# A YOCO decoder step: the cross attention's queries stored class by class instead of token by token

## The chip, the cores and the metric

The kernel runs on 1 core of one Trainium2 chip. The metric is the device time of one execution in microseconds (us). Three runs of the kernel before gave 3384.84, 3386.16 and 3391.25 us; the median is 3386.16 us.

## What is computed

The reference is one inference step of a two-layer decoder: a gated linear attention layer, then a cross attention over a shared K/V, each followed by a SwiGLU block. It is done for a prompt of 1024 tokens and for 64 sample tokens (8 sequences of 8) with the same weights. The change lies in the cross attention of the prompt, of which this is the core:

```python
WINDOWS, DILATIONS = (128, 512, 2048), (1, 4, 16)      # three groups, 16 heads each, 4 KV heads, 64 per head

def dilated_group(q, kv, start, dil, n_keys, bias):     # n_keys = window / dilation + 1 = 129
    q_pos = start + arange(Tq)
    idx = q_pos[:, None] - dil * arange(n_keys)[None, :]
    s = einsum('bqhgd,bqkhd->bqhgk', q, k[idx]) * HEAD_DIM ** -0.5
    s = where(idx >= 0, s + bias, -inf)
    p = softmax(s)
    return einsum('bqhgk,bqkhd->bqhgd', p, v[idx]), logsumexp(s)
# q = u @ w_q; the three groups' outputs are mixed with softmax weights of their logsumexp, then @ w_o
```

A query sees only keys at multiples of the dilation, so tokens fall into classes that don't see one another: in the group of dilation 4, the four classes of tokens with the same remainder by 4.

## The kernel before

All products run on TensorE (PE). A product has a left operand that is loaded into the array (LDWEIGHTS, the engine row PEld in the profile) and a right one that is streamed past it (MATMUL, row PE). Every matrix is kept as a high and a low float32r part, and a dense product is three matmuls (`mm3`, lines 164 to 170): high by high, high by low, low by high.

`cross` (line 1529) goes through twelve steps: group 2 (dilation 16), then group 1 (dilation 4), then group 0 (dilation 1), and in each the four KV heads `c`. In a step, `attend` (line 1122) computes the attention of eight tiles of 128 queries, and, woven between its stages by rates written in `cross`, side work runs: `proj_cq` (line 1037) projects the queries of the next step, `sample` serves the sample tokens of the group that was finished last, and, with group 0, `merge` mixes the groups. The order on every engine is fixed when the program is built.

**Projection.** `proj_cq` computes, for each of three token chunks `ch` (384, 384 and 320 columns, the last with 256 prompt tokens) and each half `j` of the four heads, a PSUM tile `ps` of 128 head-dimension rows by the chunk's tokens: 24 matmuls. There are two PSUM banks for these tiles (tag `mm`). The tile is then written to SBUF:
- group 2: one ScalarE (ACT) instruction, line 1060, into a float32 tile `Q` of 128 x 1024;
- groups 1 and 0: `Q` holds 512 tokens and two planes `e`, one per head. For each head ACT writes the rounded high part to its own 64 partitions (line 1070), and VectorE (DVE) writes the remainder to the other 64 (lines 1071 to 1073). One operand thus carries the high and the low part of a query, and the key tile `KT` holds the matching key rows twice.

Within a `Q` tile the tokens lie in their natural order.

**Scores.** `attend` picks the 128 queries of tile `t` out of `Q` (lines 1136, 1148, 1152) and uses them as the left operand (lines 1168, 1170, 1171):

```python
# g == 0                                     128 neighbouring columns
qv = [q[t // 4 * 2 + j][:, :, t % 4 * P:t % 4 * P + P] for j in range(2)]
# g == 1                                     every 4th column
qv = [q[2 * h + j].rearrange("p e (m r) -> p e r m", r=4)[:, :, r] for j in range(2)]
# g == 2                                     every 8th column
qv = [x.rearrange("p (m r) -> p r m", r=8)[:, t] for x in q]
```

In group 2 the prompt is cut into 8 classes of 128 tokens, and the bias masks the keys between; a score is one float32 product of 64 rows (line 1168), which the profile shows as two loads and two matmuls, for the heads `e` = 0 and 1 on the lower and the upper 64 rows of the array. A tile has four such products. In groups 1 and 0 each of the four heads has two products of 128 rows, with the two parts of the keys (lines 1170 and 1171), so eight loads to a tile, over 128 or 256 keys.

After the scores, DVE adds the bias and takes the maximum (line 1175), ACT takes the exponential (1177), PE transposes the probabilities (1200), ACT and DVE split them into `PT` (1202, 1203), PE multiplies by the values (1209), and ACT and DVE write the result (1213, 1216). The score matmuls of tile `t` stand ahead of the transposes of tile `t` - 1.

Of the kernel before, what the change touches and what calls it, by code (L numbers as in the profile page):

```python
# [7 lines left out]
F32 = mybir.dt.float32  # L8
F32R = mybir.dt.float32r
U8 = mybir.dt.uint8  # L10
AF = mybir.ActivationFunctionType
ALU = mybir.AluOpType

P = 128
# [93 lines left out]
class Kern:  # L108
# [928 lines left out]
    def proj_cq(self, u, c, g, q):  # L1037


        nc = self.nc  # L1040
        wq = [self.W.get(x) for x in self.u_cq[c, g]]

        def tile(i):
            while len(q) <= i:
                q.append(self.tl("Q", [P, SEQ]) if g == 2 else self.tl("Q", [P, 2, 512], F32R))
            return q[i]

        for ch, (t0, n) in enumerate(CH):
            n1 = min(n, SEQ - t0)
            for j in range(2):  # L1050
                ps = self.ps("gq")
                for k in range(KD):
                    w = wq[k // 4]
                    js = slice(j * P, (j + 1) * P)
                    self.mm3(ps[:, :n], (w[0][:, k % 4, js], w[1][:, k % 4, js]),
                             (u[k][ch][0][:, :n], u[k][ch][1][:, :n]), k == 0, k == KD - 1)
                    yield
                with self.tc.high_priority():
                    if g == 2:
                        nc.scalar.activation(tile(j)[:, t0:t0 + n1], ps[:, :n1], AF.Copy, scale=0.125)  # L1060
                    else:
                        for h in range(2):
                            a, b = max(t0, h * 512), min(t0 + n1, h * 512 + 512)
                            if a >= b:
                                continue
                            t = tile(2 * h + j)
                            o = slice(a - h * 512, b - h * 512)
                            for e in range(2):
                                hi, lo = slice(e * 64, e * 64 + 64), slice(64 - e * 64, 128 - e * 64)
                                nc.scalar.activation(t[hi, e, o], ps[hi, a - t0:b - t0], AF.Copy, scale=0.125)  # L1070
                                nc.vector.scalar_tensor_tensor(
                                    out=t[lo, e, o], in0=ps[hi, a - t0:b - t0], scalar=0.125,
                                    in1=t[hi, e, o].bitcast(F32), op0=ALU.mult, op1=ALU.subtract)
                    if n1 < n:
                        qn = self.tl("qn", [P, NB * NS])
                        nc.scalar.activation(qn, ps[:, n1:n], AF.Copy, scale=0.125)
                if n1 < n:
                    nc.sync.dma_start(out=self.qs[g][c][2 * j:2 * j + 2].rearrange("e d t -> (e d) t"), in_=qn)
# [43 lines left out]
    def attend(self, c, g, q, load):  # L1122


        nc = self.nc
        mm = nc.tensor.matmul
        bias = next(load)
        kv = [next(load)]
        late = None
        order = (0, 2, 4, 6, 1, 3, 5, 7) if g == 1 else range(8)  # L1130
        rs = self.tl("rs", [P, 8, 8]) if g else None
        for i, t in enumerate(order):
            if i == 1:
                kv.append(next(load))
            if g == 0:
                qv = [q[t // 4 * 2 + j][:, :, t % 4 * P:t % 4 * P + P] for j in range(2)]
                first = max(t - 1, 0)
                nk = 2 if t else 1
                if t % 4 == 0:
                    half = self.wslot("wl").rearrange("p (e n) -> p e n", e=2)  # L1140
                    st = self.tl("st", [P, 3, 4, 8])
                    for x in (1, 2):
                        nc.sync.dma_start(out=st[:, x], in_=self.sts[x][c][t * P:(t + 4) * P].rearrange("(i p) n -> p i n", p=P))
                    self.halves[c].append((half, st))
                out, dst, row = half[:, :, t % 4 * P:t % 4 * P + P], None, st[:, 0, t % 4]
            elif g == 1:
                r, h = t // 2, t % 2
                qv = [q[2 * h + j].rearrange("p e (m r) -> p e r m", r=4)[:, :, r] for j in range(2)]
                first, nk = r * 2, 1 + h
                dst, row = h * 4 + r, rs[:, h * 4 + r]  # L1150
            else:
                qv = [x.rearrange("p (m r) -> p r m", r=8)[:, t] for x in q]
                first, nk = t, 1
                dst, row = t, rs[:, t]
            w = nk * P
            if g:
                out = self.tl("row", [P, 2, P])
            pr = []
            ps = [self.ps("qk") for _ in range(2)]
            runs = [(first, nk)] if first // 4 == (first + nk - 1) // 4 else [(first, 1), (first + 1, 1)]  # L1160
            for hp in range(2):
                for e in range(2):
                    for k0, n in runs:
                        o = ps[e][:, hp * 256 + (k0 - first) * P:hp * 256 + (k0 - first + n) * P]
                        kT, ks = kv[k0 // 4][0], slice(k0 % 4 * P, (k0 % 4 + n) * P)
                        if g == 2:
                            es = slice(e * 64, (e + 1) * 64)
                            m = mm(o, lhsT=qv[hp][es], rhs=kT[es, ks], start=True, stop=True)
                        else:
                            mm(o, lhsT=qv[hp][:, e], rhs=kT[:, 0, ks], start=True, stop=False)  # L1170
                            m = mm(o, lhsT=qv[hp][:, e], rhs=kT[:, 1, ks], start=False, stop=True)  # L1171
            for hq in range(4):
                pv = ps[hq % 2][:, (hq // 2) * 256:(hq // 2) * 256 + w]
                s = self.tl("S", [P, 256])
                nc.vector.tensor_tensor_reduce(s[:, :w], pv, bias[hq][:, :w][:, ::-1], -1.0, 1e38,  # L1175
                                               ALU.add, ALU.min, row[:, hq:hq + 1])
                nc.scalar.activation(s[:, :w], s[:, :w], AF.Exp, bias=row[:, hq:hq + 1], scale=-1.0,
                                     accum_out=row[:, 4 + hq:5 + hq])
                pr.append(s)
            yield m.ins.name  # L1180
            if late:
                yield from late
            late = self.attend_out(c, g, nk, pr, [kv[k // 4][1][:, k % 4] for k in range(first, first + nk)], out, dst)
        yield from late
        if g == 1:
            nc.sync.dma_start(out=self.sts[g][c].rearrange("(h m r) n -> m h r n", h=2, r=4),
                              in_=rs.rearrange("p (h r) n -> p h r n", h=2))
        elif g == 2:
            nc.sync.dma_start(out=self.sts[g][c].rearrange("(m t) n -> m t n", t=8), in_=rs)
# [520 lines left out]
```

## Time and profile before

| | |
|---|---|
| median of three runs | 3386.16 us (3384.84 to 3391.25) |
| the profiled execution, its own time | 3382.68 us |
| its span, first to last instruction | 3380.9 us |
| PE busy | 3301.4 us, 98% |
| PEld (loads of the left operand) busy | 3141.0 us, 93% |
| DVE busy | 1644.9 us, 49% |
| ACT busy | 1219.9 us, 36% |
| cross attention, from the first score product to the last | 1629 to 2444 us |

In the profile a line is L with its number in the kernel, an operand is named without its buffer number (`aux` and `mm` are PSUM banks, `Q` the queries, `KT` the keys), and a shape is partitions by elements; the shape does not tell whether elements are neighbours. Loads and matmuls overlap, so a busy PE is not a PE at its best, and the time that one instruction takes, with its way through the pipeline, is longer than the distance from one to the next. That distance is read from the timeline, as the start of one row less the start of an earlier one. [...]

### The profile page before, as it was taken

The page shows a single profiled execution, that of the slowest core. Times are in us where ns is not written, and L with a number is a line of the kernel's source. Part 1 is how long each engine was busy: PE and PEld are TensorE (multiplying, and loading weights), DVE is VectorE, ACT ScalarE, POOL GpSimd, SP SyncE. Part 2 cuts the span into 40 slices and gives each one's busy share as a digit, 9 for nine tenths or more (in the row PEclk, how much of TensorE's full clock was granted, in tenths as well). Part 3 has the DMA queues.
Part 4 walks back from the last instruction along what each step waited for, and adds up shares of the span by engine and source line. Part 5 has one row for each costly group of instructions (what it writes and reads, how often), then busy time and mean ns, then how long its engine had stood idle before and what let it go on. Part 6 is the DMA issues. An engine that isn't in the chain of part 4 may idle for free. (4 is left out here: it accounts for less than half of the span.)

```text
span 3380.9 us, 51862 instructions
## 1 busy us (share of the span) xinstructions
PE 3301.4 (98%) x20130; PEld 3141.0 (93%) x20130; DVE 1644.9 (49%) x4041; ACT 1219.9 (36%) x3016; POOL 138.2 (4%) x138
## 2 busy tenths in 40 slices
PE   8999999999999999999999999999989999999999
PEld 7899999999999999977889999888878999999998
DVE  5666455533333333652446545767586333333335
ACT  4543344431111111332666555656654211111113
POOL 0000000100000000010000000011111000000000
PEclk9999999999999999999999988989899999999999
DMA  5122234322222222334323333434342322221202
GB/s 182 44 66 75 81 124 150 125 85 94 69 88 87 69 75 94 101 108 142 89 55 113 98 94 97 110 106 120 100 130 99 104 84 85 74 89 63 61 25 110
DMA packets 362410, 318.12 MB, mean 94 GB/s; under 512 B 91208, under 2 KB 346268, under 8 KB 360732
## 3 DMA queue, kind: packets, MB, share of 16 engines
q1 hardware_dynamic: 348472, 302.07, 28.8%
q10 hardware_dynamic: 13596, 12.34, 1.1%
q8 instruction: 158, 2.59, 0.3%
q14 instruction: 88, 0.72, 0.1%
q0 software_dynamic: 96, 0.39, 0.0%
HBM read 251.44 MB, written 107.33 MB: 106 GB/s over the span
## 5 line engine op out<-in xcount | busy, mean ns | idle before, releaser
L166 PE MATMUL aux<-u,wh 128*128 128x384 f32 (+1 forms) x2112 | 696.0, 331 | 2.5 <-ACT u L220 2.5
L169 PE MATMUL aux<-u,wh 128*128 128x384 f32 (+1 forms) x2112 | 695.4, 330 | 0.0
L170 PE MATMUL aux<-u,wl 128*128 128x384 f32 (+1 forms) x2112 | 695.0, 329 | 0.0
L166 PE MATMUL mm<-u,wh 128*128 128x384 f32 (+1 forms) x1152 | 408.8, 355 | 13.4 <-ACT u L220 11.6
L166 PEld LDWEIGHTS aux<-u,wh 128*128 128x128 f32 x2112 | 397.7, 189 | 3.5 <-ACT u L220 3.5
L169 PEld LDWEIGHTS aux<-u,wh 128*128 128x128 f32 x2112 | 397.1, 188 | 0.0
L170 PEld LDWEIGHTS aux<-u,wl 128*128 128x128 f32 x2112 | 397.1, 188 | 0.0
L169 PE MATMUL mm<-u,wh 128*128 128x384 f32 (+1 forms) x1152 | 392.8, 341 | 2.7 <-DVE u L221 2.6
L170 PE MATMUL mm<-u,wl 128*128 128x384 f32 (+1 forms) x1152 | 392.7, 341 | 0.0
L926 DVE TENSOR_TENSOR aux<-g,aux 128x384 f32<-128x384 f32 x132 | 71.3, 540 | 610.9 <-PE aux L170 422.7
L91 ACT ACTIVATE wh<-ws 128x1024 fp32r<-128x1024 f32 (+1 forms) x177 | 184.4, 1052 | 446.8 <-PE aux L169 277.6
L92 DVE TENSOR_TENSOR wl<-ws,wh 128x1024 fp32r<-128x1024 f32 (+1 forms) x177 | 214.2, 1219 | 198.9 <-ACT wh L91 198.3
L166 PEld LDWEIGHTS mm<-u,wh 128*128 128x128 f32 x1152 | 223.7, 194 | 24.4 <-ACT u L220 13.2
L169 PEld LDWEIGHTS mm<-u,wh 128*128 128x128 f32 x1152 | 223.4, 194 | 8.2 <-DVE u L221 4.2
L166 PE MATMUL mm<-h,wh 128*128 128x384 f32 (+1 forms) x704 | 230.4, 328 | 0.0
L170 PE MATMUL mm<-h,wl 128*128 128x384 f32 (+1 forms) x704 | 230.2, 327 | 0.0
L169 PE MATMUL mm<-h,wh 128*128 128x384 f32 (+1 forms) x704 | 230.2, 327 | 0.0
L170 PEld LDWEIGHTS mm<-u,wl 128*128 128x128 f32 x1152 | 223.3, 194 | 2.7 <-issue 0.2
L945 DVE TENSOR_TENSOR y<-y,mm 128x384 f32<-128x384 f32 (+1 forms) x320 | 168.5, 530 | 101.7 <-PE mm L170 101.4
L925 ACT ACTIVATE g<-aux 128x384 f32<-128x384 f32 x132 | 61.8, 468 | 432.4 <-PE aux L170 432.4
L927 ACT ACTIVATE h<-aux 128x384 fp32r<-128x384 f32 x132 | 61.9, 469 | 385.9 <-DVE aux L926 385.9
L1175 DVE CUSTOM_DVE_ANT_0 S<-aux,bias 128x128 f32<-128x128 f32 (+1 forms) x384 | 123.2, 349 | 134.6 <-PE aux L1171 58.7
(311 smaller groups left out, 6149.6 us busy)
## 6 DMA issues: line engine op xcount, KB each, us to landing
ws<-in_w_gate_up_dram SPq DMA_DIRECT2D x88, 512.0 KB
out_dram<-in_cache_win_dram SPq DMA_DIRECT2D x64, 510.0 KB
x<-in_cache_win_dram SPq DMA_DIRECT2D x48, 512.0 KB
ws<-in_w_down_dram SPq DMA_DIRECT2D x44, 512.0 KB
ws<-in_w_in_a_dram SPq DMA_DIRECT2D x24, 512.0 KB
ws<-in_w_q_b_dram SPq DMA_DIRECT2D x24, 512.0 KB
hT<-y SPq DMA_DIRECT2D x48, 192.0 KB
og<-row SPq DMA_DIRECT2D x64, 128.0 KB
```

The source lines that it names most:

```text
L91: nc.scalar.activation(v[1][:, :, :w], v[0][:, :, :w], AF.Copy)
L92: nc.vector.tensor_sub(v[2][:, :, :w], v[0][:, :, :w], v[1][:, :, :w].bitcast(F32))
L166: m = mm(out, lhsT=w[0], rhs=x[0], start=start, stop=False)
L169: mm(out, lhsT=w[0], rhs=x[1], start=False, stop=False)
L170: mm(out, lhsT=w[1], rhs=x[0], start=False, stop=stop)
L925: nc.scalar.activation(t[:, :n], pg[:, :n], AF.Silu)
L926: nc.vector.tensor_mul(pu[:, :n], t[:, :n], pu[:, :n])
L927: nc.scalar.activation(h[:, :n], pu[:, :n], AF.Copy)
L945: nc.vector.tensor_add(ys[m][c][:, :n], ys[m][c][:, :n], ps[:, :n])
L1175: nc.vector.tensor_tensor_reduce(s[:, :w], pv, bias[hq][:, :w][:, ::-1], -1.0, 1e38, ALU.add, ALU.min, row[:, hq:hq + 1])
```

## The change

The queries are written to `Q` class by class. When a projected tile leaves PSUM, the source is read with a step (every 4th column in group 1, every 8th in group 2) and the target is a block of neighbouring columns within each class; the view for group 0 has one class, so nothing changes there. `attend` then takes 128 neighbouring columns as left operand in all groups. Tile sizes, buffers, instruction counts, the order of instructions on every engine and what they wait for are the same; only the shapes of the writes of `Q` differ (128x384 becomes 128x8x48, 64x384 becomes 64x4x96, and so on). In the changed file the lines from `attend_load` on have a number higher by 4, and the three writes are lines 1061, 1074 and 1075.

```diff
                     if g == 2:
-                        nc.scalar.activation(tile(j)[:, t0:t0 + n1], ps[:, :n1], AF.Copy, scale=0.125)
+                        nc.scalar.activation(tile(j).rearrange("p (r m) -> p r m", r=8)[:, :, t0 // 8:(t0 + n1) // 8],
+                                             ps[:, :n1].rearrange("p (m r) -> p r m", r=8), AF.Copy, scale=0.125)
                     else:
                         for h in range(2):
                             a, b = max(t0, h * 512), min(t0 + n1, h * 512 + 512)
                             if a >= b:
                                 continue
-                            t = tile(2 * h + j)
-                            o = slice(a - h * 512, b - h * 512)
+                            r = 4 if g else 1
+                            t = tile(2 * h + j).rearrange("p e (r m) -> p e r m", r=r)
+                            pv = ps[:, a - t0:b - t0].rearrange("p (m r) -> p r m", r=r)
+                            o = slice((a - h * 512) // r, (b - h * 512) // r)
                             for e in range(2):
                                 hi, lo = slice(e * 64, e * 64 + 64), slice(64 - e * 64, 128 - e * 64)
-                                nc.scalar.activation(t[hi, e, o], ps[hi, a - t0:b - t0], AF.Copy, scale=0.125)
+                                nc.scalar.activation(t[hi, e, :, o], pv[hi], AF.Copy, scale=0.125)
                                 nc.vector.scalar_tensor_tensor(
-                                    out=t[lo, e, o], in0=ps[hi, a - t0:b - t0], scalar=0.125,
-                                    in1=t[hi, e, o].bitcast(F32), op0=ALU.mult, op1=ALU.subtract)
+                                    out=t[lo, e, :, o], in0=pv[hi], scalar=0.125, in1=t[hi, e, :, o].bitcast(F32),
+                                    op0=ALU.mult, op1=ALU.subtract)
...
             elif g == 1:
                 r, h = t // 2, t % 2
-                qv = [q[2 * h + j].rearrange("p e (m r) -> p e r m", r=4)[:, :, r] for j in range(2)]
+                qv = [q[2 * h + j][:, :, r * P:(r + 1) * P] for j in range(2)]
...
             else:
-                qv = [x.rearrange("p (m r) -> p r m", r=8)[:, t] for x in q]
+                qv = [x[:, t * P:(t + 1) * P] for x in q]
```

## Rows read from the trace of the kernel before

**Rows 1.** The page: span, and busy time, share and instructions of each engine

```profile
span 3380.9 us, 51862 instructions
PE 3301.4 (98%) x20130; PEld 3141.0 (93%) x20130; DVE 1644.9 (49%) x4041; ACT 1219.9 (36%) x3016; POOL 138.2 (4%) x138
```

**Rows 2.** Windows, groups 2, 1, 0: length, busy us of each engine, PEclk, DMA share, GB/s

```profile
1624.00:1812.00 188.00, 186.25 (x1081) 161.57 (x1080) 95.12 (x390) 127.64 (x434) 3.48 (x5) 1.00 0.26 63
1812.00:2122.00 310.00, 308.13 (x1863) 292.07 (x1863) 165.80 (x525) 174.22 (x541) 3.45 (x5) 0.91 0.37 105
2122.00:2450.00 328.00, 316.05 (x1943) 278.33 (x1942) 225.47 (x759) 201.31 (x610) 47.14 (x32) 0.93 0.39 110
```

**Rows 3.** Lines by form, 1624 to 1812 (group 2): busy us, mean ns | idle before, releasers

```profile
L1168 PEld LDWEIGHTS aux<-KT,Q 64*128 64x128 f32 x256 | 36.8, 325 | 10.2 <-issue 8.8 <-ACT KT L1115 1.1 <-DVE V L1109 0.3
```

**Rows 4.** Lines by form, 1812 to 2122 (group 1)

```profile
L1171 PEld LDWEIGHTS aux<-KT,Q 128*128 128x128 f32 x128 | 41.1, 328 | 0.3
L1170 PEld LDWEIGHTS aux<-KT,Q 128*128 128x128 f32 x128 | 40.7, 325 | 1.0 <-ACT KT L1118 0.3 <-ACT x L1415 0.2
```

**Rows 5.** Windows, two stretches at full clock, of group 1 and of group 0

```profile
1840.00:1900.00 60.00, 59.57 (x394) 56.95 (x394) 33.02 (x97) 34.58 (x103) 0.00 (x0) 1.00 0.43 122
2130.00:2200.00 70.00, 68.03 (x464) 61.97 (x464) 51.97 (x173) 46.68 (x146) 6.21 (x4) 1.00 0.41 115
```

**Rows 6.** Lines by form, 1840 to 1900 (group 1, every 4th column)

```profile
L1170 PEld LDWEIGHTS aux<-KT,Q 128*128 128x128 f32 x24 | 7.5, 326 | 0.2
```

**Rows 7.** Lines by form, 2130 to 2200 (group 0, neighbouring columns)

```profile
L1170 PEld LDWEIGHTS aux<-KT,Q 128*128 128x128 f32 x32 | 6.0, 190 | 0.2
```

**Rows 8.** Timeline of PEld, a tile of group 1: start us, duration us; eight loads

```profile
2082.05 0.31 PEld L1170 LDWEIGHTS aux<-KT,Q 128*128 128x128 f32 x1
...
2083.92 0.21 PEld L166 LDWEIGHTS mm<-u,wh 128*128 128x128 f32 x1
```

**Rows 9.** Timeline of PEld, a tile of group 0, eight loads

```profile
2139.70 0.19 PEld L1170 LDWEIGHTS aux<-KT,Q 128*128 128x128 f32 x1
...
2140.64 0.19 PEld L170 LDWEIGHTS mm<-u,wl 128*128 128x128 f32 x1
```

**Rows 10.** Timeline of PEld, a tile of group 2, its eight loads merged

```profile
1657.82 1.03 PEld L1168 LDWEIGHTS aux<-KT,Q 64*128 64x128 f32 x8 [0.25 <-issue]
1658.97 0.30 PEld L1209 LDWEIGHTS mx<-PT,V 128*128 128x128 f32 x2
```

**Rows 11.** Windows, two stretches at half clock, of group 1 and of group 0

```profile
1911.00:1924.00 13.00, 13.00 (x54) 12.57 (x54) 3.69 (x16) 5.25 (x18) 0.00 (x0) 0.50 0.11 30
2261.00:2265.00 4.00, 4.00 (x19) 3.98 (x19) 0.88 (x5) 0.24 (x1) 0.16 (x1) 0.50 0.66 197
```

**Rows 12.** Timeline of PEld at half clock: eight loads of group 1, three of group 0

```profile
1918.87 0.31 PEld L1170 LDWEIGHTS aux<-KT,Q 128*128 128x128 f32 x1
...
1920.73 0.31 PEld L166 LDWEIGHTS mm<-u,wh 128*128 128x128 f32 x1
...
2261.70 0.33 PEld L1171 LDWEIGHTS aux<-KT,Q 128*128 128x128 f32 x1
...
2262.34 0.97 PEld L1424 LDWEIGHTS aux<-x,x 128*128 128x128 f32 x4
```

**Rows 13.** Lines by form: writes of Q (group 2, then 1); line view: merge's products

```profile
L1060 ACT ACTIVATE Q<-mm 128x384 f32<-128x384 f32 x12 | 5.8, 486 | 1.6 <-PE mm L170 1.3
...
L1071 DVE SCALAR_TENSOR_TENSOR Q<-mm,Q 64x384 fp32r<-64x384 f32 x16 | 8.9, 555 | 2.8 <-ACT Q L1070 2.2
L1070 ACT ACTIVATE Q<-mm 64x384 fp32r<-64x384 f32 x16 | 7.7, 483 | 3.9 <-PE mm L170 3.1 <-DVE Q L1071 0.5
...
L1285 DVE TENSOR_TENSOR x<-x,aux x48: 666/684/689, 2167.4 to 2472.3; 128x512 f32<-128x512 f32 x48
```

**Rows 14.** Waits of PEld, 1624 to 1812, then 1812 to 2122: us, times, longest

```profile
PEld mx L1209 <- ACT PT L1202: 3.4, 10, 0.5
...
PEld mx L1209 <- ACT PT L1202: 1.5, 4, 0.7
```

## The prediction

> **What bounds the kernel now.** I read the page first: TensorE is busy 98% of the span and its load row 93%, while VectorE has 49% and ScalarE 36% [rows 1]. Then the windows over the three groups: in each, matmuls cover over 96% of the time (186.25 of 188, 308.13 of 310, 316.05 of 328 us), and no other engine comes near, ScalarE with 127.64 of 188 us closest [rows 2]. Then the waits of the load row: the largest wait of PE on another engine is for the probabilities' split, 3.4 us in group 2's stretch and 1.5 us in group 1's [rows 14]. So PE's own instruction stream sets the pace, and what shortens it there reaches the end, if nothing takes its place.
>
> What in that stream is slow shows in the groups by form, which set the same load side by side. A 128x128 load of queries takes 326 ns where it picks every 4th column [rows 6] and 190 ns where the columns are neighbours [rows 7], both in stretches at a granted clock of 1.00 [rows 5]. In group 2, every 8th column, a load of half the rows takes 325 ns, the whole stretch at 1.00 [rows 2, 3]. These durations overlap other work, so the price is the distance between loads, from the timeline. Eight loads of a tile of group 1 move the row on by 2083.92 - 2082.05 = 1.87 us, 0.234 us each [rows 8]; eight of group 0 by 2140.64 - 2139.70 = 0.94 us, 0.1175 us each [rows 9]. The step of the left operand costs 0.116 us per load.
>
> **The change part by part.**
>
> Group 1, loads. 256 loads (128 on each of two lines) [rows 4]. The mean clock of the stretch is 0.91 [rows 2]; with two levels, 1.00 and 0.50, 18% of the time is at half. There the gain is small: eight loads in 1920.73 - 1918.87 = 1.86 us, 0.2325 each, with the step, and three in 2262.34 - 2261.70 = 0.64 us, 0.213 each, without [rows 12], both at 0.50 [rows 11]. So 0.82 x 256 = 210 loads save 0.116 us, 24.4 us, and 46 save 0.019 us, 0.9 us. **25.3 us.**
>
> Group 2, loads. 256 loads, eight to a tile, so 32 tiles [rows 3]. In the tile shown the eight span 1.03 us to the end of the last, which takes 0.33; the last so starts 0.70 us in. If the two row halves load side by side, these are four pairs and three distances of 0.233 us, just the distance of group 1 [rows 8, 10]. The next load follows 1.15 us after the first [rows 10], 0.45 after the last pair's start. With neighbouring columns I put the distance at 0.1175 [rows 9], and take 0.14 off the tail, the difference of 325 and 190 ns [rows 3, 7]: 3 x 0.1175 + 0.31 = 0.66 us in place of 1.15. That is 0.49 us x 32 = **15.7 us.** No row shows a half-row load of neighbouring columns. Its bounds are no gain, if the distance there comes from the change between half and full rows and not from the step, and 0.49 us a tile; I take the upper end, since the distance equals group 1's.
>
> Both are on PE's own path. What is late next is the chain of ScalarE and VectorE from the scores to the transposes. A tile of group 2 lasts 188 / 32 = 5.9 us and would last 5.4; ScalarE's 127.64 us over 32 tiles is 4.0 us [rows 2]. It still fits, but waits as in [rows 14] should grow: I give back **2 us**, between 0 and 8.
>
> Group 0 and the rest. One class, so loads and writes are as before: nothing.
>
> The writes of `Q`. The same count, with a stepped read of PSUM. 486 ns for 128x384 in group 2, 483 and 555 ns on ScalarE and VectorE in group 1 [rows 13]. The nearest row is VectorE in the merge, whose 48 products read PSUM with steps of 4, 8 and 1 in equal parts and take 666 to 689 ns throughout: there the step costs at most 23 ns in 512 elements [rows 13]. For ScalarE no row shows it; I take VectorE's, nothing, and as upper bound a doubled write, 486 ns. At nothing it is covered by two banks: each stretch has 24 projected tiles (4 heads, 3 chunks, 2 halves), one per 7.8 or 12.9 us, so a bank may be held that long against 0.49 us, or 2 x (0.483 + 0.555) = 2.1 us. If that cover were gone, the writes would cost their own length. A gain is excluded, as the same elements are written.
>
> The clock. Group 1's stretch has 2 x 0.09 x 310 = 56 us at half clock [rows 2]. There, work takes 0.213 / 0.1175 = 1.8 times as long [rows 9, 12]. [...] If all of the 56 us went, the gain would be 56 x (1 - 1/1.8) = 25 us; if the clock fell more often instead, I allow a loss of 10. I take **8 us**, about a third of the upper end.
>
> The sum: 25.3 + 15.7 + 8 - 2 = 47 us off the profiled execution's 3382.68 us, 3335.7 us. That execution lies 3.5 us below the median of the runs, 3386.16, and the median is what I forecast: 3339 us.
>
> [...] The rows show two distances for loads of equal shape, 0.234 and 0.1175 us [rows 8, 9]. [...]
>
> **The rivals.**
> - *The step is not the cause.* Something else that group 1 and 2 share, the place of `Q` or the neighbours in the stream, makes the loads slow, and the change does nothing: 3386 us. For it: group 0 differs in more than the step (other side work, other key counts). Against it: at one clock and one shape the loads differ by 136 ns [rows 6, 7], and group 2 with other side work has group 1's distance [rows 8, 10].
> - *Group 2 keeps its distance.* The half-row pairs are held by something other than the step: only group 1 gains, 3339 + 15.7 = 3355 us. For it: its blocks start after an idle gap of 0.25 us that no releaser explains, 8.8 us in all [rows 3, 10]. Against it: the equal distance.
> - *ScalarE pays for the stepped read.* A doubled write costs 486 ns more for 384 columns, 1.27 ns a column. Group 2 writes 8192 columns (4 heads, 2 halves, 1024 tokens), group 1 twice that on each of two engines. ScalarE would have 10.4 and 20.7 us more to do; it has 60 and 136 us free [rows 2], so a part is hidden. If half came to lie in PE's waits, 15.5 us of the gain go: 3355 us. [...]
> - *The clock, slower than before.* PE, done sooner with its scores, waits for the exponentials, and group 1's stretch falls to half clock far more often. It is 310 us with 56 at half, so 254 + 56/1.8 = 285 us of work at full clock, 261 with group 1's loads shortened. Group 2 would still have its 15.7 us, so the whole is slower once this stretch exceeds 326 us: that is at 45% half clock, a mean of 0.78. At 0.70 it lasts 356 us, 46 more than now, and the kernel ends at 3386 + 46 - 15.7 = 3416 us. For it: the clock already falls there. Against it: PE's waits are few [rows 14], group 2's stretch stays at 1.00 and group 0's at 0.93 [rows 2].
>
> **How the numbers follow.** The forecast, both groups gain, has 0.80, with 3322 to 3352 as its own range (the clock giving 25, or nothing with 8 us of waits, 3339 + 8 + 6 = 3353). Group 2 keeping its distance has 0.08, the paid-for read 0.06, the step not being the cause 0.03, the clock 0.03. The range for 8 in 10 goes from 3322 to 3360, which takes in both cases at 3355. A measurement of this kernel can tell about 0.2%, 6.8 us. Faster: 0.80 + 0.08 + 0.06 = 0.94; no change: 0.03; slower: 0.03.
>
> **What would show it.** Right: loads at line 1172 (group 2) and lines 1174 and 1175 (group 1) near 190 ns at full clock; a tile's eight loads in about 0.94 us in group 1; group 2's stretch near 172 us, group 1's near 277; PEclk there above 0.91; the three writes of `Q` at lines 1061, 1074 and 1075 within 25 ns of now; everything after 2450 the same, only earlier. Wrong: loads that stay at 325 ns (the step is not it), group 2's distance still 0.233, ScalarE's writes well above 486 ns with PE waiting for the `mm` banks or `PT`, or a PEclk under 0.8.

## The result, and the profile after

Four runs of the changed kernel give 3348.1 us (3341.27 to 3357.14), four of the kernel before on the same chip 3385.5 us. The ratio is 0.9896, with an interval of 0.9881 to 0.9912: faster by 37 us, where 47 were forecast. The time lies in the range of the forecast, 9 us above the 3339 us that were forecast. The same kernel, timed in two further sets, gave 3345.54 us (ratio 0.9885, 0.9869 to 0.9900) and 3349.67 us (0.9902, 0.9886 to 0.9918). The profiled execution took 3352.04 us, 30.6 less than that of before.

The page of the changed kernel, span and engines, against [rows 1]:

```profile
span 3350.3 us, 51862 instructions
PE 3262.6 (97%) x20130; PEld 3095.3 (92%) x20130; DVE 1643.8 (49%) x4041; ACT 1220.1 (36%) x3016; POOL 137.3 (4%) x138
```

The same count of instructions; TensorE and its load row lose 39 and 46 us of busy time, VectorE and ScalarE keep theirs. PEclk is the mean granted clock of TensorE, as a share of full clock: 1.00 in [rows 5] and 0.50, half clock, in [rows 11]. The windows of groups 2, 1 and 0 and of the rest, cut at the same instructions as [rows 2] (length, busy us of PE, PEld, DVE, ACT, POOL, then PEclk, DMA share, GB/s):

```profile
1624.00:1800.00 176.00, 170.38 (x1084) 143.62 (x1082) 94.34 (x390) 127.53 (x436) 3.46 (x5) 1.00 0.28 67
1800.00:2087.00 287.00, 282.26 (x1863) 262.91 (x1862) 164.47 (x525) 174.08 (x541) 3.41 (x5) 0.92 0.40 114
2087.00:2419.00 332.00, 318.35 (x1941) 278.69 (x1939) 225.75 (x759) 201.99 (x611) 48.02 (x33) 0.92 0.39 109
2419.00:3350.00 931.00, 903.51 (x5454) 890.17 (x5454) 401.37 (x713) 227.40 (x431) 31.24 (x38) 0.99 0.26 84
```

Group 2 went from 188 to 176 us and group 1 from 310 to 287; group 0, which the change doesn't touch, grew from 328 to 332. The share of time that matmuls cover in group 2 fell from 186.25 of 188 to 170.38 of 176: 1.75 us uncovered became 5.6 us. In group 1 1.9 us uncovered became 4.7, in group 0 12.0 became 13.7. That is the first sign of waits that were not there.

The groups by form, first 1624 to 1800, then 1800 to 2087, answer to [rows 3, 4, 13]:

```profile
L1172 PEld LDWEIGHTS aux<-KT,Q 64*128 64x128 f32 x256 | 18.9, 186 | 10.1 <-issue 9.1 <-ACT KT L1119 1.1
L1213 PEld LDWEIGHTS mx<-PT,V 128*128 128x128 f32 x62 | 10.4, 187 | 9.1 <-ACT PT L1206 4.7 <-DVE PT L1207 2.3 <-issue 0.5
L1061 ACT ACTIVATE Q<-mm 128x384 f32<-128x384 f32 x12 | 5.8, 486 | 0.9 <-PE mm L170 0.6
...
L1174 PEld LDWEIGHTS aux<-KT,Q 128*128 128x128 f32 x128 | 26.5, 210 | 2.9 <-ACT KT L1122 1.5 <-ACT x L1419 0.4 <-DVE rs L1179 0.2
L1175 PEld LDWEIGHTS aux<-KT,Q 128*128 128x128 f32 x128 | 26.4, 212 | 1.0 <-DVE KT L1123 0.7
L1075 DVE SCALAR_TENSOR_TENSOR Q<-mm,Q 64x384 fp32r<-64x384 f32 x16 | 8.9, 555 | 3.3 <-ACT Q L1074 2.5
L1074 ACT ACTIVATE Q<-mm 64x384 fp32r<-64x384 f32 x16 | 7.8, 484 | 3.2 <-PE mm L170 2.4 <-DVE Q L1075 0.5
```

The loads of group 2 fell from 325 to 186 ns. Those of group 1 fell from 325 and 328 to 210 and 212 ns; these means still hold the loads at half clock. The writes of `Q` take 486, 555 and 484 ns where they took 486, 555 and 483. The idle time ahead of the value product's loads (line 1213) stands at 9.1 us. It stood at 6.2 before:

```profile
L1209 PEld LDWEIGHTS mx<-PT,V 128*128 128x128 f32 x62 | 10.5, 187 | 6.2 <-ACT PT L1202 3.4 <-DVE PT L1203 0.4 <-issue 0.2
```

The timeline of the load row shows both sides in single tiles. First the very tile of group 2 that the forecast was worked out on [rows 10], then that of group 1 [rows 8], at the same place of PE's order (start us, duration us):

```profile
1657.42 0.52 PEld L1172 LDWEIGHTS aux<-KT,Q 64*128 64x128 f32 x8 [0.25 <-issue]
1658.21 0.30 PEld L1213 LDWEIGHTS mx<-PT,V 128*128 128x128 f32 x2 [0.26 <-DVE PT L1207]
...
2049.61 0.19 PEld L1174 LDWEIGHTS aux<-KT,Q 128*128 128x128 f32 x1
...
2050.55 0.19 PEld L166 LDWEIGHTS mm<-u,wh 128*128 128x128 f32 x1
```

In group 1 eight loads now take 2050.55 - 2049.61 = 0.94 us, to the hundredth what group 0 took [rows 9], in place of 1.87. In group 2 the block shrank from 1.03 to 0.52 us. With pairs side by side, three distances make 0.52 - 0.19 = 0.33 us, 0.11 each, against 0.1175 forecast. But the next load follows 0.79 us after the first, not 0.66: it stands idle 0.26 us for VectorE's half of the split probabilities. In this one tile 0.36 us were gained where 0.49 were forecast: the loads did better than forecast, by 0.13 us, and 0.26 went into the wait.

**Where the time went, gap by gap.** PE executes the same 20130 matmuls in the same order, so each matmul's distance to the next can be set against the same distance in the trace of before. I sort the differences into four sums: distances next to a score product, in groups 2 and 1; all other distances of the three groups at the same granted clock in both traces; and the others where the clock differs. Beside the first profiled execution stand those of the two repeats.

| us, against the profiled run of before | forecast | first | second | third |
|---|---|---|---|---|
| group 2, at the score products | -15.7 | -16.0 | -16.0 | -16.0 |
| group 1, at the score products | -25.3 | -21.9 | -23.9 | -25.0 |
| everything else, same clock | +2 | +8.8 | +6.3 | +7.4 |
| everything else, other clock | -8 | -2.3 | -3.1 | -7.4 |
| sum | -47 | -31.4 | -36.7 | -41.0 |
| the span | | -30.6 | -36.2 | -40.4 |

Group 2's load term came as forecast, group 1's nearly. I read "everything else, same clock" as waits: in the first profile the time that no matmul covers grew by 3.9, 2.9 and 1.7 us in the three windows above, 8.4 in all. The waits cost three to more than four times what I gave back, and the clock gave a part of what I took. Of the 8.8 us of waits in the first profile, 3.6 lie in group 2, 2.7 in group 1 and 2.5 in group 0; in the repeats group 2 has 2.8 and 3.3, and group 0 only 1.0 and 0.8.

Who is waited for, in the waits (us, times, longest): the load row of the changed kernel in 1624 to 1800, then PE of the changed kernel over the whole span, then PE of before over the whole span:

```profile
PEld aux L1172 <- issue: 9.1, 37, 0.4
PEld mx L1213 <- ACT PT L1206: 4.7, 12, 0.6
PEld mx L1213 <- DVE PT L1207: 2.3, 9, 0.5
```

```profile
PE nrm L1116 <- DMA K<-kvs: 3.4, 4, 1.5
```

```profile
PE nrm L1112 <- DMA K<-kvs: 0.5, 1, 0.5
```

Two releasers have grown. The split of the probabilities, 3.4 us by ScalarE before [rows 14] and 0.4 by VectorE, is now 4.7 by ScalarE and 2.3 by VectorE. The transposes of the keys at the start of a step, which stood 0.5 us for the DMA of `K`, stand 3.4 (1.9 and 2.5 in the repeats). The 3.4 are 1.5 in the first step of group 2, 1.5 in the last step of group 0 and twice 0.2 in group 1. In the first step PE is free for the fifth transpose 7.2 us after the first, in place of 8.5, but it can start it only after 8.7: the transfer lands when it did. That wait is missing from every profile with group 2's loads as before, and stands with 0.7 to 1.9 us in every one with neighbouring loads there. In the last step of group 0, whose own work is unchanged, the wait takes 0.2 to 0.5 us in the three profiles with all of group 1's loads as before, and 0.5 to 1.6 in the nine with all of them neighbouring; why stays open. The largest idle time of the load row in group 2, 9.1 us ahead of its score loads, was 8.8 before; what it is stays open.

### The profile page after: what moved, and what is told of

It reads as the page before. It is cut to its first block, busy times and chain, and to the rows that moved or that the text cites. A ratio compares the mean times of both kernels' runs of the same rounds, so it can differ in the third digit from the quotient of the medians.

```text
span 3350.3 us, 51862 instructions
## 1 busy us (share of the span) xinstructions
PE 3262.6 (97%) x20130; PEld 3095.3 (92%) x20130; DVE 1643.8 (49%) x4041; ACT 1220.1 (36%) x3016; POOL 137.3 (4%) x138
## 4 chain that ended last, share of the span: by engine, by line
PE 47%; ACT 3%; DVE 3%; issue 2%; DMA 1%; POOL 1%; SPq 0%; DVEq 0%; ACTq 0%; POOLq 0%
PE mm L166 5%; PE mm L170 5%; PE mm L169 5%; PE aux L166 5%; PE aux L170 5%; PE aux L169 5%; PE mx L1213 2%; PE aux L154 2%; PE mx L170 1%; PE mx L169 1%; PE aux L1428 1%; PE mx L166 1%; PE mx L1204 1%; PE aux L1174 1%; PE nrm L1204 1%
```

## Experiments

**One group at a time.** Both kernels start from the changed one. The first gives group 1 back its natural order of tokens, the second group 2.

```diff
 # group 2 only
-                            r = 4 if g else 1
+                            r = 1
...
-                qv = [q[2 * h + j][:, :, r * P:(r + 1) * P] for j in range(2)]
+                qv = [q[2 * h + j].rearrange("p e (m r) -> p e r m", r=4)[:, :, r] for j in range(2)]
 # group 1 only
-                        nc.scalar.activation(tile(j).rearrange("p (r m) -> p r m", r=8)[:, :, t0 // 8:(t0 + n1) // 8],
-                                             ps[:, :n1].rearrange("p (m r) -> p r m", r=8), AF.Copy, scale=0.125)
+                        nc.scalar.activation(tile(j)[:, t0:t0 + n1], ps[:, :n1], AF.Copy, scale=0.125)
...
-                qv = [x[:, t * P:(t + 1) * P] for x in q]
+                qv = [x.rearrange("p (m r) -> p r m", r=8)[:, t] for x in q]
```

> Only group 2 is stored and read by class; group 1 as before. Theory (each group's loads lie on PE's own path, and their gains add): PE reaches the first score of group 1 about 12 us earlier than before, as in the changed kernel, group 1's loads stay 0.234 us apart, and the run ends 9 to 16 us below before, near 3373 us. Rival (the gain is one effect of the whole cross attention, such as the clock, and comes only with both): less than 5 us.

> Only group 1 is stored and read by class; group 2 as before. Theory (gains add): group 2's stretch as before, group 1's loads 0.1175 us apart at full clock, the run 18 to 30 us below before, near 3361 us; together with the run for group 2 alone about the 37 us of the whole change. Rival (one effect of the whole): clearly less than 18 us or all 37.

Group 2 alone: 3371.99 us against 3382.64, ratio 0.9964 (0.9952 to 0.9976), 10.7 us. Group 1 alone: 3358.75 us, ratio 0.9927 (0.9915 to 0.9940), 23.9 us. The loads of each follow its own part of the change and no other, by form: the kernel for group 2 in 1624 to 1800, then in 1820 to 2087;

```profile
L1172 PEld LDWEIGHTS aux<-KT,Q 64*128 64x128 f32 x256 | 18.9, 186 | 10.1 <-issue 9.1 <-ACT KT L1119 1.1
...
L1174 PEld LDWEIGHTS aux<-KT,Q 128*128 128x128 f32 x108 | 34.4, 326 | 0.7 <-ACT KT L1122 0.5
```

and the kernel for group 1 in the same windows:

```profile
L1171 PEld LDWEIGHTS aux<-KT,Q 64*128 64x128 f32 x253 | 36.1, 325 | 9.9 <-issue 8.6 <-ACT KT L1118 1.1 <-DVE V L1112 0.3
...
L1173 PEld LDWEIGHTS aux<-KT,Q 128*128 128x128 f32 x120 | 24.8, 211 | 2.3 <-ACT KT L1121 1.5 <-DVE rs L1178 0.3
```

The two gains sum to 34.6 us, the whole is 37: within the intervals they add. Group 2's 16.0 us at the score products come out as 10.7 in the time. As far as the one profile shows, there are two reasons: the waits took a part, so that its stretch, from its first score product to the first of group 1, was 12.2 us shorter (171.8 against 184.0), and the clock got no better: group 1's stretch, still with stepped loads, spent 61 us at half clock, against 55 in the profile of before and 61 in that of the writes alone, below. With neighbouring loads in group 1, on the other hand, that stretch spent between 27 and 44 us at half clock in each of nine profiles of this document. So the smaller share of half clock came with group 1's own loads.

**The writes alone and the loads alone.** The first keeps the stepped reads of PSUM and the new place of the queries, but picks the left operand as before; the second writes as before and takes 128 neighbouring columns. Both so score the wrong queries, with the same work on every engine.

```diff
 # writes only, against the changed kernel
-                qv = [q[2 * h + j][:, :, r * P:(r + 1) * P] for j in range(2)]
+                qv = [q[2 * h + j].rearrange("p e (m r) -> p e r m", r=4)[:, :, r] for j in range(2)]
...
-                qv = [x[:, t * P:(t + 1) * P] for x in q]
+                qv = [x.rearrange("p (m r) -> p r m", r=8)[:, t] for x in q]
 # loads only, against the kernel before
-                qv = [q[2 * h + j].rearrange("p e (m r) -> p e r m", r=4)[:, :, r] for j in range(2)]
+                qv = [q[2 * h + j][:, :, r * P:(r + 1) * P] for j in range(2)]
...
-                qv = [x.rearrange("p (m r) -> p r m", r=8)[:, t] for x in q]
+                qv = [x[:, t * P:(t + 1) * P] for x in q]
```

> The queries are written class by class, but the scores still take every 4th or 8th column as left operand, so they are computed with the wrong queries. Theory (the stepped read of PSUM costs nothing): writes of Q at 483 to 486 and 555 ns for 384 columns, and the time is that of before within 0.2%, 3379 to 3392 us. Rival (the writes take part of the gain back, 5 us or more through PE's waits): 3391 us or more.

> The queries are written in natural order as before, but the scores take 128 neighbouring columns, so they are computed with the wrong queries. Theory (only the loads matter): the time of the changed kernel within 0.2%, 3341 to 3355 us. Rival (the stepped writes take part of the gain back): 5 us or more below the changed kernel, 3343 us or less as a median, with PE's waits for the probabilities' split as few as before.

Writes alone: 3384.16 us over 12 runs, ratio 1.0008 (0.9997 to 1.0018). Loads alone: 3351.39 us, ratio 0.9902 (0.9886 to 0.9919), the changed kernel's own. The writes' kernel by form, 1624 to 1800, then 1820 to 2087:

```profile
L1172 PEld LDWEIGHTS aux<-KT,Q 64*128 64x128 f32 x254 | 36.3, 325 | 9.9 <-issue 8.6 <-ACT KT L1119 1.1 <-DVE V L1113 0.3
L1061 ACT ACTIVATE Q<-mm 128x384 f32<-128x384 f32 x12 | 5.8, 486 | 1.6 <-PE mm L170 1.3
...
L1075 DVE SCALAR_TENSOR_TENSOR Q<-mm,Q 64x384 fp32r<-64x384 f32 x16 | 8.9, 555 | 2.8 <-ACT Q L1074 2.2
L1074 ACT ACTIVATE Q<-mm 64x384 fp32r<-64x384 f32 x16 | 7.8, 484 | 3.9 <-PE mm L170 3.1 <-DVE Q L1075 0.5
```

The whole gain is the loads', and the stepped read of PSUM is free: on ScalarE with steps of 4 and 8 (484 and 486 ns), on VectorE with a step of 4 (555 ns). Nor do the new writes cause the new waits: with the loads alone, the distances elsewhere grew by much the same 3.7, 2.7 and 2.4 us in groups 2, 1 and 0.

**How the price grows with the step.** Group 1's four classes take left operands with steps of 1, 2, 3 and 4 columns, group 2's eight tiles steps of 1 to 8, each on a source line of its own.

```diff
-                            m = mm(o, lhsT=qv[hp][es], rhs=kT[es, ks], start=True, stop=True)
+                            lq = q[hp][es, :P * (t + 1)].rearrange("p (m s) -> p s m", s=t + 1)[:, 0]
...
+                            sx = t // 2 + 1
+                            lq = q[2 * (t % 2) + hp][:, e, :P * sx].rearrange("p (m s) -> p s m", s=sx)[:, 0]
```

> As the changed kernel, but the left operand takes every s-th column, s = 1 to 8 by the tile in group 2 and s = 1 to 4 by the class in group 1, so the scores are computed with the wrong queries; each s has a line of its own. [...] Rival (any step other than 1 costs all of it): 325 ns from s = 2 on. Second rival (the cost grows with the distance): longer at s = 8 than at s = 4.

Its one run took 3365.70 us, 17 less than the profiled run of before; the rows are what it was made for. The timeline of the load row in group 1 has a tile of each step within 28 us. For each, the first of its eight loads and the first load after them:

```profile
1985.16 0.19 PEld L1198 LDWEIGHTS aux<-KT,Q 128*128 128x128 f32 x1
...
1986.11 0.19 PEld L166 LDWEIGHTS mm<-u,wh 128*128 128x128 f32 x1
...
1991.30 0.20 PEld L1201 LDWEIGHTS aux<-KT,Q 128*128 128x128 f32 x1
...
1992.25 0.19 PEld L166 LDWEIGHTS mm<-u,wh 128*128 128x128 f32 x1
...
2001.80 0.26 PEld L1204 LDWEIGHTS aux<-KT,Q 128*128 128x128 f32 x1
...
2003.19 0.20 PEld L154 LDWEIGHTS aux<-sc,x 128*128 128x128 f32 x1
...
2010.64 0.31 PEld L1207 LDWEIGHTS aux<-KT,Q 128*128 128x128 f32 x1
...
2012.49 0.21 PEld L166 LDWEIGHTS mm<-u,wh 128*128 128x128 f32 x1
```

The window over them shows that all four ran at full clock:

```profile
1985.00:2013.00 28.00, 27.99 (x194) 26.42 (x194) 15.80 (x50) 15.78 (x49) 0.00 (x0) 1.00 0.25 78
```

Eight loads take 0.95 us with step 1, 0.95 with step 2, 1.39 with step 3 and 1.85 with step 4: 0.119, 0.119, 0.174 and 0.231 us each. Beyond step 4, the durations of group 2's half-row loads tell, by form (line 1174 is step 1, 1176 step 2, 1178 step 3, 1180 step 4, 1184 step 6, 1188 step 8):

```profile
L1188 PEld LDWEIGHTS aux<-KT,Q 64*128 64x128 f32 x32 | 4.7, 325 | 1.0 <-issue 1.0
L1184 PEld LDWEIGHTS aux<-KT,Q 64*128 64x128 f32 x32 | 4.5, 306 | 1.9 <-issue 1.9
L1180 PEld LDWEIGHTS aux<-KT,Q 64*128 64x128 f32 x32 | 4.0, 321 | 1.0 <-issue 1.0
L1178 PEld LDWEIGHTS aux<-KT,Q 64*128 64x128 f32 x32 | 3.6, 255 | 1.4 <-issue 1.4
L1176 PEld LDWEIGHTS aux<-KT,Q 64*128 64x128 f32 x32 | 2.7, 193 | 0.6 <-issue 0.6
L1174 PEld LDWEIGHTS aux<-KT,Q 64*128 64x128 f32 x32 | 2.4, 186 | 1.4 <-ACT KT L1119 1.1 <-issue 0.3
```

186 and 193 ns for steps 1 and 2, 255 for step 3, 321 for step 4, and no more with 6 or 8 (306 and 325). The place of the tile in the step does not make the difference: before, with one step for all, group 2's loads took between 308 and 333 ns. Nor is the price one of distance, 325 ns at step 8 against 321 at step 4, nor the same for every step, 193 ns at step 2. Why step 2 adds nothing to the 0.119 us of step 1, and step 3 about half of what step 4 adds (0.055 and 0.112 us), was not shown. Types other than float32 were not run, nor steps 2 and 3 that start at another column.

**Is the new wait ScalarE's, and can it be covered?** In group 2 the value product waits for the split probabilities. Two remedies: one more slot of the projection between a tile's transposes and its value product, with the rate of the side work set to the new count of slots; and group 2's writes of `Q` on VectorE, so that ScalarE has 5.8 us less to do for the 384-column tiles, 8.9 with the others.

```diff
 # more cover
             yield m.ins.name
+            if g == 2:
+                yield m.ins.name
...
-            steps = 24 if g == 2 else 32
+            steps = 32
 # write on VectorE
-                        nc.scalar.activation(tile(j).rearrange("p (r m) -> p r m", r=8)[:, :, t0 // 8:(t0 + n1) // 8],
-                                             ps[:, :n1].rearrange("p (m r) -> p r m", r=8), AF.Copy, scale=0.125)
+                        nc.vector.tensor_scalar(tile(j).rearrange("p (r m) -> p r m", r=8)[:, :, t0 // 8:(t0 + n1) // 8],
+                                                ps[:, :n1].rearrange("p (m r) -> p r m", r=8), 0.125, 0.0, ALU.mult, ALU.add)
```

The changed kernel itself ran beside them as the mark.

> The changed kernel as it is, beside the runs of the next two, with the granted clock of each run. Theory (the change shortens the loads, and the clock falls to half less often by some 10 us): 34 to 40 us below before, mean clock 0.001 to 0.002 above before's, which is 7 to 13 us less at half clock. Rival (the clock's part is chance): the same mean clock as before within 0.0005, and a gain of 30 us or less.

> The changed kernel, with a further slot of projection work between the transposes and the value product in group 2 (four slots a tile in place of three, at 1.5 steps each in place of 2). Theory (the part of group 2's gain that was given back are waits for the split of the probabilities): those waits fall from 4.7 and 2.3 us to under 2, and group 2's stretch is 2 to 4 us shorter than in the changed kernel; the rest the same. Rival (the waits are of another kind, or only move to the transposes): group 2's stretch within 1 us.

> The changed kernel, with the queries of group 2 written by VectorE in place of ScalarE. Theory (ScalarE's queue, busy for over 70% of that stretch, is what PE waits for): ScalarE has 11 us less to do there, PE's waits for the split shrink, and group 2's stretch is 1 to 3 us shorter than in the changed kernel. Rival (it is the length of the chain, not the load): within 1 us, with waits for VectorE in place of those for ScalarE.

The mark gave 3345.54 us, 36.8 below before, with a mean clock of its runs of 0.9805 against 0.9790: as expected. More cover gave 3338.99 us (3333.65 to 3356.26), ratio 0.9878 (0.9857 to 0.9900); the write on VectorE 3343.4 us, 0.9882 (0.9868 to 0.9895). All three intervals overlap. Both expectations had group 2's stretch shorter; in neither profile it was: 171.6 us with cover and 173.5 with the write on VectorE, 3.4 us of each at half clock, against 170.7 of the mark at full clock throughout. Yet the write on VectorE did shorten the waits for the split, 1624 to 1800:

```profile
PEld mx L1213 <- ACT PT L1206: 3.8, 10, 0.6
PEld mx L1213 <- DVE PT L1207: 1.0, 2, 0.5
```

That is 4.8 us against 6.9 of the mark. So ScalarE's writes are a part of what delays the split, some 2 us. But PE's waits for the DMA of `K` in the first two steps of group 2 grew from 0.7 to 2.9 us: about as much as was won at the split was lost at the keys. The cover's profile of this set has 5.0 us of waits for the split (1.5 for ScalarE, 3.5 for VectorE) where under 2 was expected, and 3.0 at the keys of group 2. Since 6.5 us between the medians left it open whether the cover pays, I ran it again, alone and with the other.

> The changed kernel unaltered, on the same chip as the next two: 3341 to 3351 us, as its two medians so far (3348.1 and 3345.5 us); it is the mark that the two variants are held against.

> The kernel with one more slot of the projection between the transposes and the value product of group 2, a second time. If the waits for PT in group 2 are what is left to win there (6 to 8 us of TensorE's idle time in that stretch, of which the slot took some 2 us in the first look), the median lies 2 to 6 us below that of the changed kernel. If the slot only moves the wait to another place, the two medians lie within 2 us and the 6.5 us between them so far were the clock's.

> The extra slot of the projection and group 2's writes of Q on VectorE together. If ScalarE's 5.8 us of writes in group 2 delay the split of the probabilities, both parts add up and the median lies 4 to 8 us below the changed kernel's. If the writes lie in time that ScalarE has free, this one equals the kernel with the extra slot alone, within 2 us.

The mark: 3349.67 us (3342.27 to 3355.48), 32.3 below before, with a mean clock of 0.9790 against 0.9787: this time the clock's part is all but gone. Cover: 3340.51 us (3327.47 to 3346.57), ratio 0.9868 (0.9848 to 0.9887). Both: 3343.39 us (3341.63 to 3345.69), ratio 0.9883 (0.9865 to 0.9901). What the cover does to the wait stands in the row of the value product's loads, 1624 to 1800:

```profile
L1215 PEld LDWEIGHTS mx<-PT,V 128*128 128x128 f32 x64 | 10.8, 187 | 7.1 <-DVE PT L1207 3.4 <-ACT PT L1206 1.8 <-PE mm L170 0.3
```

7.1 us in place of 9.1; ScalarE's part falls from 4.7 to 1.8 and VectorE's rises from 2.3 to 3.4. Group 2's stretch is 169.7 us, against 171.3 of the mark. With both sets together, 11 runs with cover have a mean of 3339.7 us and the mark's 10 a mean of 3347.4: 7.8 us less, and in both sets the median was lower, by 6.5 and 9.2. It is the fastest version that was run. But only 1 to 2 us of that are seen in the wait, and the runs with cover had the higher granted clock, 0.9815 against 0.9796 in the mean. An estimate from a straight line through time and clock of these 21 runs, with one slope for both kernels, gives 2.8 us to each 0.001 of mean clock: 5.3 of the 7.8 us go with the clock, and 2.5 are left for the cover, which fits the wait. Why the clock would be better, or whether it only was so in these runs, stays open. With the two remedies together the waits for the split fall further, to 1.4 and 2.4 us, but the time is no lower than with the cover alone, so no gains add up in it; whether the two are equal within 2 us the scatter does not tell.

## Why the prediction was right, and where it was off

- **What bounds the kernel** was read rightly: PE's own stream. The load of the left operand was made shorter, and the end came earlier, by four fifths of the sum.
- **The step as the cause.** Shown by the loads alone, which have the whole gain, and by the kernel with eight steps. "The step is not the cause" falls: 0.119, 0.174 and 0.231 us for the same 128 columns.
- **Group 2's loads**, 15.7 us from an assumed pair distance: 16.0 in each profile. The half-row load, of which no row of before showed a neighbouring case, has the distance of the whole one (0.11 us, against 0.119 in group 1). "Group 2 keeps its distance" falls with 0.52 us for a block of 1.03.
- **Group 1's loads**, 25.3 us: 21.9 to 25.0, depending on how many of them met half clock. There the step indeed costs almost nothing: of the distances between two score loads that were at half clock in both traces, 20 together lost 0.3 us, while 159 at full clock lost 17.9.
- **The writes**, nothing: 1.0008 with an interval that holds 1, and 486, 555 and 484 ns. "ScalarE pays for the stepped read" falls. Its upper bound, a doubled write, was far off; the nearest row, VectorE's merge, was right for ScalarE too.
- **The waits given back**, 2 us: the step that failed. They came to 8.8, 6.3 and 7.4 us. The reasoning was by ScalarE's mean load in group 2, 4.0 of 5.4 us to a tile, which still fits. But a tile's split has to come between its transposes and its value product, and a mean over a tile says nothing about that place: the tile shown above lost 0.26 us there to VectorE, which has only half of its time taken, but whose half of the split comes after ScalarE's (it waits 15.5 us for it in that stretch). That the place counts is borne out by the cover, which cut ScalarE's part from 4.7 to 1.8 us; that ScalarE's load counts too, by its writes, some 2 us. I also sized it in group 2's split alone: 0.7 to 1.5 us went there to the DMA of `K`, which did not land sooner when PE was (8.7 us after the first transpose, with PE free at 7.2), and groups 1 and 0 lost 1 to 3 us each. The upper bound, 8, was about right.
- **The clock**, 8 us: my estimate, about a third of the 25 us that a stretch without half clock would give, and no run shows this term; the three profiles gave 2.3, 3.1 and 7.4 in its place, and by the mean clocks of the later two sets it comes in one and not in the other. Group 1's stretch did spend less at half clock (44 us in the first profile, 55 before), but group 0's, which was to stay as it was, spent more: 48 us before, 51, 58 and 51 after. "The clock, slower than before" falls, with 0.92 in group 1 against 0.91.
- Together, in the mean of the three profiles: 5.5 us of waits too few, 3.7 us of clock too many and 1.7 us of group 1's loads too many make up the 11 us between the forecast 47 and their 36. All three lie on the same side, so no luck helped; the wide range took them in. Two slips of the sums changed nothing: the upper end of the forecast's own range is 3353, not 3352, and at full clock group 1's 256 loads would save 30 us, not the 24 that stand in the rival of the slower clock. In the list of what would show it, group 2's stretch was to be near 172 us and was 176, group 1's near 277 and was 287 (about 280 in both repeats), and after group 0 all was the same, only earlier: 931 against 930 us.

## What to carry to other kernels

Where an engine's own stream sets the pace, look at its loads by form and set the distances of equal shapes beside each other: here the shape in the profile was the same and only the step of the operand differed, and with it the distance, by a factor of two (0.231 us at step 4, 0.119 at step 1). Put the step where a slack engine reads PSUM, here 484, 486 and 555 ns with it and 483, 486 and 555 without, not where TensorE loads, and measure the load at its own step: here one of two float32 columns took 0.119 us, as neighbouring columns did, and would have needed no change at all. When a stream of one engine is made denser, cost the waits at the place where it takes the others' results, tile by tile, and go through the stretches that the change does not touch as well: transfers and splits that just arrived in time here did so no more (in the first profile 3.4 us of waits for `K` in place of 0.5, and in group 2 7.0 for the split in place of 3.8).

## What the runs showed of the hardware

- The load of a left operand of 128 float32 columns takes 0.119 us of the stream at steps 1 and 2, 0.174 at step 3, 0.231 at step 4. The durations of group 2's half-row loads show the same ladder (186, 193, 255, 321 ns), and that 6 and 8 (306, 325) cost no more than 4. I had expected only that a step costs.
- Two loads on the two halves of the rows go side by side with or without a step: those of a pair start within 0.01 us of each other, and four pairs of neighbouring columns take 0.52 us, 0.11 from one to the next.
- Reads of PSUM with a step take as long as neighbouring ones: ScalarE's with steps of 4 and 8 float32, 484 against 483 and 486 against 486 ns, VectorE's with a step of 4, 555 against 555.
- The scatter of this kernel's runs goes with the granted clock: the four runs of the changed kernel at mean clocks of 0.983, 0.982, 0.979 and 0.977 took 3341.27, 3344.15, 3352.04 and 3357.14 us.
